# Weight remainders by an accumulating DMA onto a negated rounded copy, and their products last in a tile

## The chip, the cores and the metric

One Trainium2 chip, one of its cores. The time is that of one execution of the whole kernel on the device, in microseconds (us), a median over runs. The engines are called PE (TensorE, the matrix engine, whose weight loads are listed as PEld), DVE (VectorE), ACT (ScalarE), POOL (GpSimd) and SP (SyncE, which issues DMA transfers).

## What is computed

Two layers of a diffusion backbone over 512 latent and 256 context tokens of width 1024. Each layer modulates and normalises its input, projects it once, runs three groups of heads on it (latent attention, neighbourhood attention, a gated DeltaNet that begins with a convolution), projects back, and ends with a gated MLP of hidden width 2816. The last layer keeps only the latent tokens from its mixers on.

```python
h = modulate(rms_norm(x, g_mix[l]), mx[:, 0], mx[:, 1])
mq, mkv, mpe, nq, nk, nv, dn = split_in(h @ w_in[l])
...
x = x + mx[:, 2] * (jnp.concatenate([mla_o, na_o, dn_o], axis=-1) @ w_out[l])
h = modulate(rms_norm(x, g_ffn[l]), mx[:, 3], mx[:, 4])
x = x + mx[:, 5] * swiglu(h, w_gate[l], w_up[l], w_down[l])

def swiglu(h, w_gate, w_up, w_down):
    return (jax.nn.silu(h @ w_gate) * (h @ w_up)) @ w_down
```

Everything is float32.

## The kernel before

PE multiplies in a rounded float32 format (F32R). To keep float32 accuracy each operand is split in two: a rounded copy (hi) and the remainder (lo = value - hi). A product is then three: hi x hi, hi x lo and lo x hi. For weights W and activations X the code calls them wh·xh, wh·xl and wl·xh.

Weights stream through `wtiles` (L202 to L214), one tile of up to 128 x 1024 a call, 208 calls in the program: 48 for the input projection (`w_in`), 4 for the attention's values (`w_nav`), 88 for gate and up (`w_gu`), 48 for the down projection (`w_dn`), 20 for the output projection. A call loads the raw tile (`wr`, two buffers) by a DMA that SP issues, rounds it on ACT into `wh` (L212) and subtracts on POOL into `wl` (L213). `wh` and `wl` have two buffers each; some tiles lie in buffers of their own, `kh` and `kl`. Two tiles of the input projection (`WV`, L48) are subtracted on DVE instead.

`gemm` (L337 to L346) multiplies such a tile: for each set of tokens and each of its (mostly eight) 128-row slices the three products follow one another, wh·xh, wh·xl, wl·xh, all into one accumulator. `proj` (L386) calls it for the input projection's tiles, for one set of tokens at a time. The MLP goes through the hidden width in three parts (`FFN_PARTS`, 8, 7 and 7 blocks of 128). For each block there are a gate and an up tile (accumulators `acc_gu`), then ACT's silu (L1336), DVE's multiplication (L1339), ACT's rounding into `ah` (L1342) and DVE's remainder `al` (L1343). Behind a part's blocks come eight down tiles (`acc_d`), which DVE adds to the residual stream (L1357). In layer 1 a set has 512 tokens, so a gate, up or down tile of 8 slices is 24 matmuls of 128x512.

The DeltaNet's convolution (`conv`) copies an accumulator with borders into `xp` (borders cleared on POOL, L485 to L490), adds four shifted copies on DVE (L497), takes a tanh on ACT (L499) and writes keys, values or queries on DVE (L500, L502, `dn_k` for the keys).

The order on each engine is set by a scheduler with its own simulated times (L1453), not by the order of the code. Each engine then works through its row; an instruction that has to wait holds up all behind it on that engine. A buffer is written again only when its last readers are through.

Of the kernel before, what the change touches and what calls it, by code (L numbers as in the profile page):

```python
# [29 lines left out]
# the last rows of the last down projection: their weights stay for one set of tokens after the other  # L30
# [17 lines left out]
WV = ((6,), (23,))  # L48
# [77 lines left out]
def emit(ctx, tc, a, out, dbg=None):  # L126
# [20 lines left out]
    # the constants: those for the first norm, and the rest, which is loaded behind the first modulation weights  # L147
# [8 lines left out]
    # the first five again for single-pass products, in which they are exact  # L156
# [22 lines left out]
    def preload(after):  # L179
        """the table with both exp and ln, behind the last user of another one"""  # L180
        with tc.issue_after(after.ins):
            S.preload_act_table_set("natural_log_exp_and_others")

    # silu(c), silu(c_ctx), padded to 32 stationary columns
# [3 lines left out]
    # the same as rows  # L188
# [13 lines left out]
    def wtiles(src, n, slot=None, bufs=None, eng=G):  # L202
# [10 lines left out]
        eng.tensor_tensor(out=lo[:, sl], in0=raw[:, sl], in1=hi[:, sl].bitcast(F32), op=ALU.subtract)  # L213
        return hi[:, sl], lo[:, sl]  # L214

    def ada_cols(l, part, j0, nb, bank, sb, slot):
        """nb * 128 modulation rows on the tensor engine: the two conditions stay, the weights stream;
        a quarter of the terms in each column group, summed and turned at the end"""
# [20 lines left out]
    def ada_rows(todo, sb, after):  # L239
        """modulation vectors on the vector engine, one block of 128 rows per step"""  # L240
# [62 lines left out]
    def open_norm(l, side):  # L303
        """the tiles of the input projection's operand, and a set of tokens normed at a time"""
        o = K()
        o.es_h, o.es = ExitStack(), ExitStack()
        hp = pool(o.es_h, f"h{l}", side=side)
        o.hh, o.hl = [[hp.tile([P, T], F32R, name=f"h{x}{k}") for k in range(KD)] for x in "hl"]
        o.sb = pool(o.es, f"sb_n{l}", 2, side=side)
        return o  # L310

    def next_norm(l, xT, bank, side):
        """one set of tokens a step: the norm of the next layer, or the last one"""
# [23 lines left out]
    def gemm(acc, wh, wl, xh, xl, sts, c0=0):  # L337
        """acc[:, st] = W^T x for a [P, nk*128] weight tile over nk activation tiles"""
        nk = len(xh)
        for st in sts:  # L340
            for k in range(nk):
                w = slice(k * P, (k + 1) * P)
                o = acc[:, st.start - c0:st.stop - c0]
                mm(nc, o, wh[:, w], xh[k][:, st], k == 0, False)
                mm(nc, o, wh[:, w], xl[k][:, st], False, False)
                mm(nc, o, wl[:, w], xh[k][:, st], False, k == nk - 1)  # L346

    # ------------------------------------------------------------------ layers
# [10 lines left out]
def layer(tc, nc, a, l, es_x, xT, env, nx):  # L359
# [8 lines left out]
    # the normed input and the residual stream lie on one side, the mixers' data on the other  # L368
# [17 lines left out]
    def proj(t, ctx_too=True, sets=(LAT, CTX)):  # L386
        w, res = early.pop(t, None) or (wtiles(a["w_in"][l, t], 1024, eng=V if t in WV[l] else G), [])
# [20 lines left out]
    else:  # L408
        # the latent tokens of the first projections go ahead of the norm of the context
# [13 lines left out]
    # ------------------------------------------------ input projection  # L423
# [26 lines left out]
    # the latents of the latent attention, split  # L450
# [6 lines left out]
    # bias tables of a pair of heads with the window mask, per kind of query block: [(r c), j, kind, b, kr, c]  # L457
# [49 lines left out]
    # a, b and the rotary key  # L507
# [9 lines left out]
    # ------------------------------------------------ gated DeltaNet: gates and triangular blocks  # L517
# [30 lines left out]
    # cumulative decays  # L548
# [15 lines left out]
    def norms(nm, t_, stat, rk, w_ctx):  # L564
        """sums of squares of q or k per token, and the root's inverse"""
# [34 lines left out]
    # per chunk: Gram matrices and decays; leaves -L packed (forward above the diagonal, backward below)  # L600
    # and the keys decayed to the end of the chunk; the decays wait for the queries where the
    # neighbourhood attention's will be
# [43 lines left out]
    def att_in(x, sb):  # L646
        """the attention matrices of a chunk"""
# [12 lines left out]
    def base_inverse(sb):  # L660
        """(I + L)^-1 of the diagonal 32-blocks, one block per partition: rows of the transposed inverses"""
# [17 lines left out]
    # ------------------------------------------------ the rest of the input projection  # L679
# [14 lines left out]
    # neighbourhood attention: keys, queries (latent ones in blocks of 16 grid columns), values  # L694
# [21 lines left out]
    def do_nav():  # L716
# [13 lines left out]
        # latent values again in blocks of 16 grid columns (r, c): at starts 0, 16, 32, 48 and 8, 24, 40  # L730
# [9 lines left out]
    # the key/value latent is normalised here  # L740
# [15 lines left out]
    # query latent; its row scale is applied to the scores  # L756
    def do_ql():
# [13 lines left out]
        # sml[:, 0:6] = scale * rstd_q per token, sml[:, 6:12] its negative  # L771
# [8 lines left out]
    # 2 silu(z) of the output gate  # L780
# [41 lines left out]
    # ------------------------------------------------ neighbourhood attention, beside the last of the input projection  # L822
# [84 lines left out]
    def inverse(x0, sb, eb):  # L907
        """transposed inverses of two chunks for both directions, joined from 32-blocks: forward and backward
        off-diagonal blocks lie in disjoint places and share the products"""
# [548 lines left out]
```

## Time and profile before

| | us |
|---|---|
| median of 3 runs | 2159.58 |
| lowest and highest | 2149.07, 2163.1 |
| span of the profiled execution | 2157.6 |

| engine | busy us in the profiled execution | share |
|---|---|---|
| PE | 2006.2 | 93% |
| DVE | 1244.7 | 58% |
| POOL | 839.5 | 39% |
| ACT | 708.0 | 33% |

A busy share is an average over stages that have different limits. By the names at work the span divides so (in us from its start): modulation and first norms up to 54; input projection and the DeltaNet's preparation 54 to 378; the rest of the mixers, with the attention heads in 486 to 702; layer 0's MLP 702 to 1242; then layer 1 the same way, 1242 to 1512, 1620 to 1788, 1788 to 2147, and the final norm. A line of the trace gives how long an instruction ran; what stands in square brackets behind it is how long the engine sat idle before, and what released it.

### The profile page before, as it was taken

What the parts mean: (1) busy time and instruction counts of PE and PEld (TensorE: products, weight loads), DVE (VectorE), ACT (ScalarE), POOL (GpSimd) and SP (SyncE); (2) the same over time, 40 slices, a digit from 0 to 9 for tenths busy, and PEclk for the clock granted to TensorE, in tenths of its full rate; (3) what the DMA queues carried; (4) which work ended last, traced back from release to release, by engine and by line L of the source; (5) the groups of instructions that cost most, each with busy time, mean ns of one, the idle gap of its engine ahead of it and who ended that gap; (6) DMA issues with size and microseconds to landing.
All of it is one profiled execution on the core that took longest, in us unless ns stands there. A gap on an engine that the chain in (4) does not pass through costs nothing. (4 is left out here: it accounts for less than half of the span.)

```text
span 2157.6 us, 32133 instructions
## 1 busy us (share of the span) xinstructions
PE 2006.2 (93%) x12770; PEld 1685.9 (78%) x12770; DVE 1244.7 (58%) x2107; ACT 708.0 (33%) x1381; POOL 839.5 (39%) x602
## 2 busy tenths in 40 slices
PE   6899888998999999999999988877999889999998
PEld 4778667887787888888888866766887778888887
DVE  4888963667757457246353368898478753212123
ACT  5433223334534221121122344222434543222233
POOL 3466563103323232322232443856412352444444
PEclk9999998999999999999999999988799999999999
DMA  7424252543312335334432331332523232333332
GB/s 275 81 81 148 72 142 85 156 149 120 103 55 88 108 119 167 97 127 139 125 117 84 128 76 59 124 107 83 132 65 93 72 105 61 98 90 94 100 96 91
DMA packets 119278, 232.57 MB, mean 108 GB/s; under 512 B 30484, under 2 KB 55956, under 8 KB 119000
## 3 DMA queue, kind: packets, MB, share of 16 engines
q1 hardware_dynamic: 119128, 230.51, 35.2%
q8 instruction: 101, 1.65, 0.3%
q14 instruction: 49, 0.40, 0.1%
HBM read 199.46 MB, written 31.01 MB: 107 GB/s over the span
## 5 line engine op out<-in xcount | busy, mean ns | idle before, releaser
L213 POOL TENSOR_TENSOR wl<-wr,wh 128x1024 fp32r<-128x1024 f32 (+2 forms) x188 | 440.6, 2344 | 711.5 <-ACT wh L212 708.5
L212 ACT CAST wh<-wr 128x1024 fp32r<-128x1024 f32 (+2 forms) x190 | 193.5, 1019 | 733.5 <-PE acc_gu L104 285.5
L104 PE MATMUL acc_gu<-fl,wh 128*128 128x512 f32 (+1 forms) x1024 | 360.6, 353 | 5.3 <-DVE fl L301 5.3
L104 PE MATMUL acc_gu<-fh,wh 128*128 128x512 f32 (+1 forms) x1024 | 358.3, 353 | 6.1 <-ACT fh L300 5.3
L104 PE MATMUL acc_gu<-fh,wl 128*128 128x512 f32 (+1 forms) x1024 | 360.1, 352 | 0.0
L104 PE MATMUL acc_in<-hh,wh 128*128 128x512 f32 (+1 forms) x640 | 229.9, 363 | 19.3 <-ACT xp L487 7.7
L104 PE MATMUL acc_in<-hh,wl 128*128 128x512 f32 (+1 forms) x640 | 226.8, 358 | 20.4 <-POOL wl L213 20.4
L104 PE MATMUL acc_in<-hl,wh 128*128 128x512 f32 (+1 forms) x640 | 229.7, 360 | 3.1 <-DVE hl L301 2.0
L1339 DVE TENSOR_TENSOR av<-acc_gu,av 128x768 f32<-128x768 f32 (+1 forms) x44 | 36.3, 825 | 335.8 <-PE acc_gu L104 329.3
L104 PEld LDWEIGHTS acc_gu<-fl,wh 128*128 128x128 f32 x1024 | 193.6, 189 | 34.3 <-DVE fl L301 6.2
L104 PEld LDWEIGHTS acc_gu<-fh,wh 128*128 128x128 f32 x1024 | 192.6, 189 | 35.0 <-ACT fh L300 6.9
L104 PEld LDWEIGHTS acc_gu<-fh,wl 128*128 128x128 f32 x1024 | 193.8, 189 | 27.7
L104 PEld LDWEIGHTS acc_in<-hh,wh 128*128 128x128 f32 x640 | 125.2, 197 | 44.9 <-ACT xp L487 9.4
L104 PE MATMUL acc_d<-al,wh 128*128 128x512 f32 (+1 forms) x444 | 158.0, 356 | 0.0
L104 PE MATMUL acc_d<-ah,wh 128*128 128x512 f32 (+1 forms) x444 | 157.9, 356 | 0.0
L104 PE MATMUL acc_d<-ah,wl 128*128 128x512 f32 (+1 forms) x444 | 156.8, 355 | 0.0
L104 PEld LDWEIGHTS acc_in<-hh,wl 128*128 128x128 f32 x640 | 124.6, 196 | 40.5 <-POOL wl L213 22.5
L250 DVE CUSTOM_DVE_ANT_0 junk<-wada,scb 128x1024 f32<-128x1024 f32 x112 | 145.1, 1295 | 6.9 <-DMA wada<-w_adaT 4.1
L104 PEld LDWEIGHTS acc_in<-hl,wh 128*128 128x128 f32 x640 | 125.8, 197 | 26.4 <-DVE hl L301 4.6
L497 DVE SCALAR_TENSOR_TENSOR cy<-xp,cw,cy 128x770 f32<-128x770 f32 (+1 forms) x96 | 126.0, 1312 | 22.1 <-ACT cy L495 18.4
L1357 DVE SCALAR_TENSOR_TENSOR xT<-acc_d,mod,xT 128x512 f32<-128x512 f32 (+1 forms) x76 | 46.5, 635 | 157.1 <-PE acc_d L104 157.1
L1343 DVE TENSOR_TENSOR al<-av,ah 128x768 fp32r<-128x768 f32 (+1 forms) x44 | 100.5, 2284 | 35.1 <-ACT ah L1342 35.1
(389 smaller groups left out, 4032.2 us busy)
## 6 DMA issues: line engine op xcount, KB each, us to landing
wr<-w_gu SPq DMA_DIRECT2D x88, 512.0 KB, 3.6
wada<-w_adaT SPq DMA_DIRECT2D x56, 512.0 KB, 3.4
wr<-w_in SPq DMA_DIRECT2D x48, 512.0 KB, 3.5
wr<-w_dn SPq DMA_DIRECT2D x32, 448.0 KB, 3.4
wada<-w_ada SPq DMA_DIRECT2D x24, 512.0 KB, 3.4
wada<-w_ada SPq DMA_DIRECT2D x8, 1024.0 KB, 8.7
wr<-w_dn SPq DMA_DIRECT2D x16, 512.0 KB, 3.6
xT<-xT SPq DMA_DIRECT2D x16, 384.0 KB, 5.1
```

Source lines behind the costliest of these rows:

```text
L104: nc.tensor.matmul(out, lhsT, rhs, start=start, stop=stop)
L212: S.copy(out=hi[:, sl], in_=raw[:, sl])
L213: eng.tensor_tensor(out=lo[:, sl], in0=raw[:, sl], in1=hi[:, sl].bitcast(F32), op=ALU.subtract)
L250: V.tensor_tensor_reduce(out=junk, in0=w, in1=scb[:, s], scale=1.0, scalar=0.0, op0=ALU.mult, op1=ALU.add, accum_out=mod[l][:, part, j, s: ...
L497: stt(out=y[:, :wid], in0=xp[:, j:j + wid], scalar=w_(j), in1=y[:, :wid], op0=ALU.mult, op1=ALU.add)
L1339: tt(out=av[:, :nT], in0=accs[1][:, :nT], in1=av[:, :nT], op=ALU.mult)
L1343: after.append(tt(out=l_[:, :nT], in0=av[:, :nT], in1=h_[:, :nT].bitcast(F32), op=ALU.subtract))
L1357: stt(out=xT[:, m, st_], in0=acc, scalar=mod[l][:, 5, m, s:s + 1], in1=xT[:, m, st_], op0=ALU.mult, op1=ALU.add)
```

## The change

`wtiles` rounds on ACT as before. The remainder is then made in two steps: ACT writes the rounded copy's source once more into the `wl` buffer, in the rounded format and times -1, so that it holds -hi; and a DMA that POOL issues reads the weights from memory a second time and adds them to it, which leaves value - hi. `gemm` now takes all products with `wh` of all its sets of tokens first, and those with `wl` behind them. The choice of an engine for the subtraction (`eng`, `WV`) is gone. Comments that the diff also drops are not shown.

```diff
@@ wtiles
-    def wtiles(src, n, slot=None, bufs=None, eng=G):
+    def wtiles(src, n, slot=None, bufs=None):
...
         S.copy(out=hi[:, sl], in_=raw[:, sl])
-        eng.tensor_tensor(out=lo[:, sl], in0=raw[:, sl], in1=hi[:, sl].bitcast(F32), op=ALU.subtract)
+
+        S.activation(out=lo[:, sl], in_=raw[:, sl], func=AF.Copy, scale=-1.0)
+        G.dma_start(out=lo[:, sl], in_=src, accum_op=ALU.add)
         return hi[:, sl], lo[:, sl]
@@ gemm
         nk = len(xh)
-        for st in sts:
+        W = [slice(k * P, (k + 1) * P) for k in range(nk)]
+        os_ = [(acc[:, st.start - c0:st.stop - c0], st) for st in sts]
+        for o, st in os_:
             for k in range(nk):
-                w = slice(k * P, (k + 1) * P)
-                o = acc[:, st.start - c0:st.stop - c0]
-                mm(nc, o, wh[:, w], xh[k][:, st], k == 0, False)
-                mm(nc, o, wh[:, w], xl[k][:, st], False, False)
-                mm(nc, o, wl[:, w], xh[k][:, st], False, k == nk - 1)
+                mm(nc, o, wh[:, W[k]], xh[k][:, st], k == 0, False)
+                mm(nc, o, wh[:, W[k]], xl[k][:, st], False, False)
+        for o, st in os_:
+            for k in range(nk):
+                mm(nc, o, wl[:, W[k]], xh[k][:, st], False, k == nk - 1)
@@ proj
-        w, res = early.pop(t, None) or (wtiles(a["w_in"][l, t], 1024, eng=V if t in WV[l] else G), [])
+        w, res = early.pop(t, None) or (wtiles(a["w_in"][l, t], 1024), [])
```

What the scheduler makes of it shows in the rows of the engines. On PE, in layer 1's MLP, before: `acc_gu` is an accumulator, `fh` and `fl` are the slices of the normed activations, and the number behind a name is that of the tile. The end of one gate/up tile and the start of the next:

```order
L104 MATMUL acc_gu_17850<-fl7_16168,wh_17845 128x512
L104 MATMUL acc_gu_17850<-fh7_16160,wl_17846 128x512
L104 MATMUL acc_gu_17881<-fh0_16153,wh_17876 128x512 [waits DVE_49,Activation_49]
L104 MATMUL acc_gu_17881<-fl0_16161,wh_17876 128x512
L104 MATMUL acc_gu_17881<-fh0_16153,wl_17877 128x512 [waits Pool_49]
L104 MATMUL acc_gu_17881<-fh1_16154,wh_17876 128x512
```

The same engine and place now:

```order
L103 MATMUL acc_gu_18108<-fh7_16300,wh_18102 128x512
L103 MATMUL acc_gu_18108<-fl7_16308,wh_18102 128x512
L103 MATMUL acc_gu_18037<-fh0_16293,wl_18032 128x512 [waits DMASW2_49]
L103 MATMUL acc_gu_18037<-fh1_16294,wl_18032 128x512
L103 MATMUL acc_gu_18037<-fh2_16295,wl_18032 128x512
...
L103 MATMUL acc_gu_18037<-fh7_16300,wl_18032 128x512
L103 MATMUL acc_gu_18140<-fh0_16293,wh_18134 128x512 [waits DVE_49,Activation_49]
```

A tile's eight `wl` products (18037) now stand behind the sixteen `wh` products of the tile after it (18108), and wait for a DMA instead of POOL. In layer 0's MLP they stand behind the `wh` products of their own tile.

On ACT, in the same stage, before (`av` is the silu of a gate tile, `ah` the rounding of its product with the up tile):

```order
L212 CAST wh_17876<-wr_17875 128x1024 [waits DMAHW6_49,PE_49,Pool_49]
L212 CAST wh_17914<-wr_17913 128x1024 [waits DMAHW7_49,PE_49,Pool_49]
L1336 ACTIVATE av_17906<-acc_gu_17850 128x512 [waits PE_49]
L212 CAST wh_17945<-wr_17944 128x1024 [waits DMAHW0_49,PE_49,Pool_49]
L1342 CAST ah_17909<-av_17906 128x512 [waits DVE_49]
```

And now:

```order
L211 CAST wh_18134<-wr_18133 128x1024 [waits DMAHW0_49,Activation_49]
L1340 ACTIVATE av_18094<-acc_gu_18037 128x512 [waits PE_49]
L213 ACTIVATE wl_18103<-wr_18101 128x1024 [waits DMASW2_49]
L211 CAST wh_18173<-wr_18172 128x1024 [waits DMAHW1_49,Activation_49]
L213 ACTIVATE wl_18135<-wr_18133 128x1024 [waits DMASW3_49,PE_49]
L1346 CAST ah_18097<-av_18094 128x512 [waits DVE_49]
```

A negated copy (L213) stands behind each rounding, and waits until PE is through with the tile that had the buffer before. The silu of a gate tile stands ahead of one of them.

On POOL, in layer 0's input projection, before (`gul` belongs to the DeltaNet's gates, `xp` is the convolution's input):

```order
L627 TENSOR_TENSOR gul_992<-cst2_61,g_l_960 128x512
L485 MEMSET xp_813 128x2 [waits DVE_49,Activation_49,Pool_49]
L486 MEMSET xp_813 128x2
L490 MEMSET xp_813 128x2
L213 TENSOR_TENSOR wl_1011<-wr_1009,wh_1010 128x1024 [waits DMAHW0_49,PE_49,Activation_49]
L485 MEMSET xp_885 128x2 [waits DVE_49,Activation_49,Pool_49]
```

And now:

```order
L631 TENSOR_TENSOR gul_997<-cst2_61,g_l_965 128x512
L489 MEMSET xp_817 128x2 [waits DVE_49,Activation_49,Pool_49]
L490 MEMSET xp_817 128x2
L494 MEMSET xp_817 128x2
L214 DMA wl_1016<-w_in 128x1024 [waits DMASW3_49,Activation_49]
L489 MEMSET xp_890 128x2 [waits DVE_49,Activation_49,Pool_49]
```

The issue of the accumulating DMA has the place that the subtraction had.

## Rows read from the trace of the kernel before

**Rows 1.** The page's head and its first section: busy time by engine.

```profile
span 2157.6 us, 32133 instructions
PE 2006.2 (93%) x12770; PEld 1685.9 (78%) x12770; DVE 1244.7 (58%) x2107; ACT 708.0 (33%) x1381; POOL 839.5 (39%) x602
```

**Rows 2.** Windows by stage: start:end, length, busy time (instructions) per engine, granted clock, DMA.

```profile
core 0: us, PE busy (x) PEld busy (x) DVE busy (x) ACT busy (x) POOL busy (x), PEclk, DMA share, GB/s
54.00:378.00 324.00, 286.41 (x1793) 241.79 (x1792) 243.00 (x344) 103.39 (x180) 172.95 (x149) 0.93 0.36 102
486.00:702.00 216.00, 196.03 (x1256) 161.04 (x1254) 149.99 (x312) 98.72 (x251) 69.36 (x55) 0.94 0.28 91
702.00:1242.00 540.00, 540.00 (x3122) 472.55 (x3121) 254.05 (x342) 117.57 (x136) 163.04 (x73) 1.00 0.39 121
1242.00:1512.00 270.00, 224.91 (x1161) 181.54 (x1160) 216.62 (x300) 90.55 (x153) 156.29 (x136) 0.92 0.31 90
1620.00:1788.00 168.00, 149.47 (x1020) 125.77 (x1020) 117.89 (x240) 79.65 (x211) 58.83 (x53) 0.96 0.28 85
1788.00:2147.00 359.00, 359.00 (x1672) 298.79 (x1671) 96.97 (x95) 106.23 (x149) 155.00 (x72) 1.00 0.30 90
```

**Rows 3.** Waits of PE: who waited for whom, us in total, times, longest.

```profile
PE acc_in L104 <- POOL wl L213: 20.4, 5, 9.0
```

**Rows 4.** The page's costliest groups: the subtraction; count | busy, mean ns | idle before, releaser.

```profile
L213 POOL TENSOR_TENSOR wl<-wr,wh 128x1024 fp32r<-128x1024 f32 (+2 forms) x188 | 440.6, 2344 | 711.5 <-ACT wh L212 708.5
```

**Rows 5.** Windows by stage of line 213 alone, the subtraction: DVE, then POOL.

```profile
54.00:378.00 324.00, 1.22 (x1) 57.45 (x23) 0.93 0.36 102
486.00:702.00 216.00, 0.00 (x0) 30.55 (x14) 0.94 0.28 91
1242.00:1512.00 270.00, 0.00 (x0) 53.25 (x22) 0.92 0.31 90
1620.00:1788.00 168.00, 0.00 (x0) 26.01 (x12) 0.96 0.28 85
1788.00:2147.00 359.00, 0.00 (x0) 148.76 (x64) 1.00 0.30 90
```

**Rows 6.** Timeline of DVE, 82 to 110 us: start, duration, instruction, idle before.

```profile
81.42 0.69 DVE L500 SCALAR_TENSOR_TENSOR dn_k<-th,cy 128x512 f32<-128x512 f32 x1 [1.89 <-ACT th L499]
...
90.49 2.37 DVE L500 SCALAR_TENSOR_TENSOR dn_k<-th,cy 128x512 f32<-128x512 f32 x1 [0.92 <-ACT th L499]
...
98.28 0.69 DVE L500 SCALAR_TENSOR_TENSOR dn_k<-th,cy 128x512 f32<-128x512 f32 x1 [0.91 <-ACT th L499]
```

**Rows 7.** Timeline of POOL in the same stretch.

```profile
89.91 2.40 POOL L213 TENSOR_TENSOR wl<-wr,wh 128x1024 fp32r<-128x1024 f32 x1
```

**Rows 8.** Timeline of POOL in layer 1's MLP, two tiles.

```profile
1843.85 2.39 POOL L213 TENSOR_TENSOR wl<-wr,wh 128x1024 fp32r<-128x1024 f32 x1 [3.06 <-ACT wh L212]
1849.29 2.39 POOL L213 TENSOR_TENSOR wl<-wr,wh 128x1024 fp32r<-128x1024 f32 x1 [3.05 <-ACT wh L212]
```

**Rows 9.** Timeline of ACT in the same stretch.

```profile
1842.72 1.05 ACT L212 CAST wh<-wr 128x1024 fp32r<-128x1024 f32 x1 [3.84 <-PE acc_gu L104]
1843.68 0.59 ACT L1336 ACTIVATE av<-acc_gu 128x512 f32<-128x512 f32 x1
```

**Rows 10.** Timeline of DVE in the same stretch.

```profile
1848.42 0.69 DVE L1339 TENSOR_TENSOR av<-acc_gu,av 128x512 f32<-128x512 f32 x1 [7.07 <-PE acc_gu L104]
1849.80 2.44 DVE L1343 TENSOR_TENSOR al<-av,ah 128x512 fp32r<-128x512 f32 x1 [0.69 <-ACT ah L1342]
```

**Rows 11.** DMA issues of the page: count, KB each, median us from issue to landing.

```profile
wr<-w_gu SPq DMA_DIRECT2D x88, 512.0 KB, 3.6
```

**Rows 12.** Line 213 by form: durations in ns (least/median/most), first and last start.

```profile
L213 DVE TENSOR_TENSOR wl<-wr,wh x2: 1220/1222/1225, 66.6 to 1518.5; 128x1024 fp32r<-128x1024 f32 x2
```

**Rows 13.** Chain that ended last, in order of time: a stretch of gate/up matmuls, start, length.

```profile
1914.87 76.18 PE acc_gu L104 x336
```

More of the change, by code (lines that the diff above doesn't have):

```diff
@@ L47 @@
 INV = ((3, 4), (5, 2))
-WV = ((6,), (23,))
 MR = 2
```

## The prediction, made before the changed kernel ran

> **What bounds the kernel now.** I read the busy shares first [rows 1]: PE is at work 93% of 2157.6 us, so about 151 us are left in which another engine can matter. Next the same by stage [rows 2]. In the two gated-MLP stages (702 to 1242 and 1788 to 2147) PE is busy all the time; the reader is to see that nothing can be gained there, only lost. In the two stages of the input projection and the DeltaNet preparation (54 to 378 and 1242 to 1512) PE is idle for 37.6 and 45.1 us, and the engine busy most beside it is DVE, 243.0 of 324 and 216.6 of 270 us (0.75 and 0.80). The two attention stages leave 20.0 and 18.5 us of PE idle with DVE at 0.69 and 0.70. Last the waits of PE [rows 3]: 20.4 us for the subtracted remainder, in five waits, the largest single entry.
>
> The subtraction itself is cheap to look at: 188 of them, 2.34 us each, with POOL idle 711.5 us ahead of them, nearly all of it for ScalarE's rounding [rows 4]. POOL as an engine is no bound. What the subtraction does to others is seen where DVE meets it [rows 6, 7]: the same DVE instruction (128x512 into `dn_k`) takes 0.69 us at 81.42 and at 98.28, but 2.37 us at 90.49, and in between POOL subtracts from 89.91 to 92.31. DVE was held up by 1.68 us and went on when POOL was done.
>
> **What the change removes.** Per tile one POOL subtraction. In the two DVE-heavy stages there are 23 + 22 = 45 of them [rows 5]. A DVE instruction that comes at a random moment of a 2.4 us subtraction is held up by half of it, 1.2 us, and DVE has work at hand for about 0.78 of the time, so one subtraction costs DVE 1.2 x 0.78 = 0.94 us, and 45 cost 42 us. Bounds: nothing (DVE catches up while it would wait anyway), and 45 x 1.68 = 76 us, which is about all that PE idles there. I take two thirds of 42, 28 us, since DVE sets the pace in most of these stages but not at their beginnings. In the attention stages 14 + 12 = 26 subtractions cost DVE 26 x 1.2 x 0.69 = 21.5 us; there the softmax chain goes round several engines, and I take one third, 7 us. In the MLP stages DVE is slack and its relief is worth nothing.
>
> **What it adds on ScalarE.** One more pass per tile, as long as the rounding, 1.05 us [rows 9]: 208 x 1.05 = 218 us on an engine that is busy 708 of 2157.6 us [rows 1]. Between the units of the MLP it is hidden by idle time: three ScalarE instructions there leave 3.8 us of every 5.44 free. In the DVE-heavy stages it stands ahead of the `tanh` for which DVE waits 0.9 us at a time [rows 6]: 45 x half of 1.05 x ScalarE's share 0.33 x the same two thirds comes to 5 us.
>
> **What it adds on the DMA.** Each tile is now read a second time, by a DMA that POOL issues and that adds into the negated copy. No row of before shows such a DMA. Its duration D, from issue to landing, is bounded by rows: below by the plain load of 512 KB, 3.6 us [rows 11]; above by three of these one after the other (read the source, read the destination, write), 10.8 us. I take 3.6, plus the same bytes moved once more for the destination, plus the same again because the next raw load runs beside it. One load fills all the engines for 0.30 x 5.44 = 1.6 us (share of the last MLP stage [rows 2], one tile in 5.44 us [rows 8]), so D = 3.6 + 1.6 + 1.6 = 6.8 us, nearer to the lower bound.
>
> **What it moves.** The wl products stand after all wh products of their tile, and in layer 1's MLP after those of the next tile too, so D has room. A matmul takes 76.18 / 336 = 0.2267 us [rows 13]. There are two wl buffers: from the end of one tile's wl products to the start of those that use the same buffer again, PE goes through wh of a tile (16), wl of another (8), wh of the next (16), 40 x 0.2267 = 9.07 us. The negated copy takes 1.05 of them, and before it the silu of a gate tile 0.59 [rows 9]. So D may be 8.0 us, or 7.4 behind a silu, and 6.8 fits: cost 0. Without that cover the price is steep: a buffer's round is copy 1.05, D, and its own wl products 8 x 0.2267 = 1.81, for two tiles. Past D = 8.0 each us more costs half a us for each of 64 tiles [rows 5], 32 us. Layer 0's MLP has 768 tokens per tile and so half as much room again.
>
> Two places get less cover. At the change from gate/up to down in the second and third part of layer 1, only two matmuls stand between the last gate/up product and the first that needs `al`; DVE's multiply and its remainder are 0.69 and up to 2.44 us [rows 10], so about 2 us each, 4 us in all, up to 9. And the 20.4 us of waits for wl [rows 3]: the DMA is later than POOL was (6.8 against 2.4), but wl is needed 16 matmuls, 3.6 us, later. I leave them as they are.
>
> POOL's issues: behind them stand the clearing of `xp`'s borders and the small products of the gates, which waited for ScalarE behind the subtraction already. POOL's own 440 us go away; what writing a DMA's description costs it no row shows, and I bound it by 0 and the 2.34 us that it replaces, off the path in either case. SP issues what it did.
>
> **A rule that speaks against it.** DVE's and POOL's mutual hold-up [rows 6, 7] is the row. The Trainium skill, "SBUF — State Buffer", section "SBUF: two separate sides", says that a DMA issued from the GpSimd queue has its descriptors written by GpSimd, which cannot write them while VectorE runs an operation in a two-port mode, so that the transfer seems blocked by that operation; no DMA in this trace comes from that queue, so no run here shows it yet.
>
> **The sum.** 28 + 7 gained, 5 and 4 lost: 26 us. The profiled execution's span is 2157.6, about 2 us under the median of 2159.6: 2157.6 - 26 + 2 = 2133.6 us.
>
> **The rivals.** *B, the accumulating DMA paces layer 1's MLP.* If adding costs three passes, D is 10.8: the round is 1.05 + 10.8 + 1.81 = 13.66 for two tiles, 6.83 each against 5.44, 64 x 1.39 = 89 us lost there: 2133.6 + 89 = 2223. It eats the whole gain of 26 from D = 8.8 on. For it: the transfer is the one thing not seen, and PE has no slack there. Against it: the engines are only 0.30 busy [rows 2], and all moved bytes doubled or tripled still fit. Chance 0.26. *C, DVE's hold-up is not on the path.* The stages idle for chains (conv, norm, gates), and DVE makes up for it; then only the 7 us, less 9 of costs: 2162. For it: of PE's waits only some name DVE, and the longest names POOL, whose replacement is longer. Chance 0.17. *D, DVE holds up POOL's DMAs.* The DMA that falls on the `al` remainder, one in two gate/up tiles, comes up to 2.44 us late [rows 10]: D = 9.2, the round 12.1 for two tiles against 10.88, 1.2 us for each of about 20 pairs, 24 us: 2133.6 + 24 = 2158. Against it: 2.44 us is itself a remainder that met a subtraction (POOL from 1849.29, DVE from 1849.80 [rows 8, 10]); DVE takes 1.22 us for twice the width [rows 12], so it would shrink to about 0.6. Chance 0.09. [...]
>
> **How the numbers follow.** My forecast has 0.48, with its own range 2095 (all of the 42 + 21.5 comes back) to 2150. A measurement here tells about 1% from no change: 2138 and 2181. Faster: the forecast's part below 2138, 0.42. Same: its rest 0.06, most of C and half of D, and a mild B, 0.30. Slower: the rest of B, C and D, 0.28. The range goes from 2095 to B's 2225.
>
> **What would show it.** Right: in the stages 54 to 378 and 1242 to 1512 DVE's conv instructions at their short durations, both stages shorter by some 14 us each, `al` near 0.6 us, the last MLP stage still 359 us with PE full, and the DMA landing within 8.0 us. Wrong: PE waiting for the DMA into wl in the last MLP stage, landings above 8.0 us there, or the two DVE-heavy stages as long as before with DVE now idle.

## The result, and the profile after

The changed kernel takes 2235.1 us (median of 4 runs, 2225.59 to 2238.8) against 2160.7 for the kernel before on the same chip: 1.036 times as long, 95% interval 1.0329 to 1.0382. The forecast was 2133.6 us in a range of 2095 to 2225. It was wrong in sign, and the time lies above the range. (The 2160.7 is a median of 4 runs, the three shown ahead of the prediction and one more.) One execution, 2207.9 us of e10 below, ran in a slower state of the chip at a granted clock of 0.944 and is left out.

The head of the page after, its first section, the queue of POOL's DMAs and the issues of the gate/up weights:

```profile
span 2230.7 us, 32485 instructions
PE 2044.9 (92%) x12770; PEld 1697.6 (76%) x12770; DVE 1112.8 (50%) x2105; ACT 902.8 (40%) x1589; POOL 530.3 (24%) x604
q0 software_dynamic: 29952, 104.87, 26.9%
wr<-w_gu SPq DMA_DIRECT2D x88, 512.0 KB, 3.9
wl<-w_gu POOLq DMA_DIRECT2D x84, 512.0 KB, 7.8
```

Beside [rows 1], DVE has lost 132 us of busy time, POOL 309, and ACT has gained 195, all as meant; yet the span is 73 us longer. The accumulating DMA takes 7.8 us from issue to landing where 6.8 was forecast. PE has the same 12770 products as before and is busy 39 us longer with them.

Where the time went is read from windows cut at the first gate/up product and the last down product of each layer. Of the kernel before, then of the changed one (columns as in [rows 2]):

```profile
0.00:682.00 682.00, 605.86 (x4575) 501.19 (x4576) 470.21 (x914) 260.94 (x600) 270.82 (x242) 0.95 0.38 118
682.00:1239.00 557.00, 555.45 (x3178) 484.19 (x3178) 271.84 (x368) 123.03 (x149) 164.74 (x74) 0.99 0.39 123
1239.00:1772.00 533.00, 474.66 (x3295) 392.18 (x3293) 388.94 (x708) 208.51 (x466) 238.78 (x207) 0.93 0.32 91
1772.00:2147.00 375.00, 368.80 (x1723) 307.75 (x1722) 109.50 (x113) 113.58 (x165) 161.78 (x76) 0.99 0.30 89
```

```profile
0.00:692.00 692.00, 609.89 (x4574) 501.72 (x4574) 439.25 (x913) 296.34 (x640) 212.19 (x244) 0.95 0.54 145
692.00:1249.00 557.00, 555.39 (x3177) 484.44 (x3178) 230.01 (x367) 190.47 (x214) 64.15 (x73) 1.00 0.73 184
1249.00:1794.00 545.00, 488.77 (x3295) 401.17 (x3293) 370.92 (x708) 242.44 (x507) 186.11 (x211) 0.90 0.50 123
1794.00:2220.00 426.00, 389.44 (x1724) 309.68 (x1724) 68.49 (x113) 171.85 (x226) 64.86 (x76) 0.97 0.71 157
```

Layer 0's MLP is as long as before. Layer 1's MLP is 50 us longer, and the two stretches ahead of the MLPs, where 35 us were to be gained, are 10 and 12 us longer, although DVE has 49 us less to do in them.

PE loses this time in two ways, by standing idle and by working more slowly. In layer 1's MLP it idles 30 us more than before (length less busy time) and is busy 21 us more. In the stretch ahead of that MLP it idles 56 us, before 58; its 3295 products take 14 us longer, at a mean granted clock of 0.90 against 0.93. How the two ways hang together is seen at one place (timeline of PE in the changed kernel, first part of layer 1's MLP): PE idles 4.0 us for an accumulating DMA, and the eight products behind it, at 1878.52, take 3.79 us where eight such take 2.0 to 2.1. The granted clock from 1878.5 to 1884 is 0.50, the lower (1.2 GHz) of its two levels. There the wait cost more than its own length. How much of the 39 us comes about in this way was not followed.

What paces the second and third part of layer 1's MLP stands on the chain of work that ended last (start, length, what):

```profile
1963.24 1.06 ACT wl L213
1964.30 0.02 issue
1964.32 5.07 DMA wr<-w_gu
...
1969.49 1.04 ACT wh L211
1970.53 0.50 ACT av L1340
1971.03 0.96 ACT wl L213
...
1972.00 3.92 DMA wr<-w_gu
...
1976.95 1.06 ACT wl L213
...
1978.03 3.72 DMA wr<-w_gu
```

Neither PE nor the accumulating DMA is in it. The negated copy of one tile ends, 20 ns later a raw load starts, the rounding follows the landing, the next negated copy follows the rounding, and the next load follows that. In the chain of before this stretch was matmuls alone [rows 13]. The rows on ACT, printed with the change, say why. The copies of `wr_18101` and `wr_18133` are of neighbouring tiles, and between them stands the rounding of `wr_18172`, the tile after both. That tile has to be loaded into the buffer that the first copy sets free, and the second copy can't overtake the rounding that waits for this load. So the two raw buffers never load at the same time; they work as one. Copies start at 1963.24, 1970.93 and 1976.95, 6.9 us apart on average and 6.3 over the whole second part (1944.3 to 2025.9, 13 tiles), where PE's products of a tile take 5.44.

In the first part of the same MLP it is the accumulating DMA that the chain goes through:

```profile
1855.37 7.92 DMA wl<-w_gu
...
1863.34 2.12 PE acc_gu L103 x8
...
1865.49 3.59 issue
...
1869.09 9.38 DMA wl<-w_gu
...
1878.52 3.79 PE acc_gu L103 x8
...
1884.28 8.11 DMA wl<-w_gu
```

That is the prediction's round of a wl buffer (DMA, its eight products, silu and copy), here 13.7 and 15.2 us for two tiles against 10.88. The 3.59 us that the chain calls issue hold more than silu and copy: a rounding stands ahead of them on ACT, and it had waited until 1866.20 for its raw load.

### The profile page after: what moved, and what is told of

It is laid out like the page before. It is cut to its first block, busy times and chain, and to the rows that moved or that the text cites. A ratio compares the mean times of both kernels' runs of the same rounds, so it can differ in the third digit from the quotient of the medians.

```text
span 2230.7 us, 32485 instructions
## 1 busy us (share of the span) xinstructions
PE 2044.9 (92%) x12770; PEld 1697.6 (76%) x12770; DVE 1112.8 (50%) x2105; ACT 902.8 (40%) x1589; POOL 530.3 (24%) x604
## 3 DMA queue, kind: packets, MB, share of 16 engines
q0 software_dynamic: 29952, 104.87, 26.9%
## 4 chain that ended last, share of the span: by engine, by line
PE 57%; DMA 16%; DVE 12%; issue 6%; ACT 6%; POOL 1%; SPq 1%; DVEq 0%; ACTq 0%; POOLq 0%
PE acc_gu L103 18%; PE acc_d L103 10%; PE acc_in L103 7%; PE acc_o L103 5%; DMA wr<-w_gu 4%; DVE cy L501 2%; DMA wl<-w_gu 2%; DMA wl<-w_dn 2%; ACT wl L213 2%; DVE tmp L677 2%; PE pp L103 1%; PE s_mla L103 1%; PE o_mla L103 1%; PE s_na L103 1%; DMA wl<-w_in 1%
## 5 line engine op out<-in xcount | busy, mean ns | idle before, releaser
L103 PE MATMUL acc_gu<-fh,wh 128*128 128x512 f32 (+1 forms) x1024 | 348.1, 357 | 23.2 <-ACT wh L211 12.6
L103 PE MATMUL acc_gu<-fl,wh 128*128 128x512 f32 (+1 forms) x1024 | 344.7, 355 | 0.0
L103 PEld LDWEIGHTS acc_gu<-fh,wh 128*128 128x128 f32 x1024 | 194.1, 190 | 61.7 <-ACT wh L211 23.2
L213 ACT ACTIVATE wl<-wr 128x1024 fp32r<-128x1024 f32 (+2 forms) x190 | 194.9, 1026 | 93.9 <-PE acc_gu L103 51.1
L103 PE MATMUL acc_in<-hh,wh 128*128 128x512 f32 (+1 forms) x640 | 219.8, 363 | 14.1 <-ACT wh L211 5.4
L103 PE MATMUL acc_in<-hl,wh 128*128 128x512 f32 (+1 forms) x640 | 218.8, 360 | 3.8 <-POOL hl L299 2.4
L103 PE MATMUL acc_gu<-fh,wl 128*128 128x512 f32 (+1 forms) x1024 | 210.0, 354 | 8.3 <-DMA wl<-w_gu 8.2
L214 POOL DMA_DIRECT2D wl<-w_gu x84 | 73.1, 870 | 573.7 <-ACT wl L213 525.6
L103 PEld LDWEIGHTS acc_gu<-fh,wl 128*128 128x128 f32 x1024 | 169.1, 189 | 39.4 <-DMA wl<-w_gu 11.8
L103 PE MATMUL acc_in<-hh,wl 128*128 128x512 f32 (+1 forms) x640 | 143.4, 365 | 15.1 <-DMA wl<-w_in 15.1
L103 PEld LDWEIGHTS acc_in<-hh,wl 128*128 128x128 f32 x640 | 110.0, 202 | 36.3 <-DMA wl<-w_in 17.7
L677 POOL TENSOR_TENSOR tmp<-R,Bk 96x1 f32<-96x1 f32 (+30 forms) x62 | 84.9, 1369 | 82.0 <-DVE R L678 71.5
```

Of the source, the lines that this page charges most:

```text
L103: nc.tensor.matmul(out, lhsT, rhs, start=start, stop=stop)
L213: S.activation(out=lo[:, sl], in_=raw[:, sl], func=AF.Copy, scale=-1.0)
L214: G.dma_start(out=lo[:, sl], in_=src, accum_op=ALU.add)
L677: (V if d == 0 else G).tensor_tensor(out=t_, in0=R[:, d, js, js], in1=bc1(Bk[:, js, i], s), op=ALU.mult)
```

## The experiments

Each ran beside the kernel before on the same chip, where that took 2156.6 to 2157.2 us (2160.7 beside the changed kernel); the ratio is to that. Changing the source also lets the scheduler order the rows anew, so only e6, whose rows stayed in the same order, differs from its parent in one thing alone. Lengths of the four stretches (start to layer 0's MLP, that MLP, from there to layer 1's MLP, that MLP), in us, by the first gate/up and last down products of one profiled execution each:

| kernel | to MLP 0 | MLP 0 | to MLP 1 | MLP 1 | time, median | ratio to before (95%) |
|---|---|---|---|---|---|---|
| before | 681.8 | 557.0 | 532.8 | 375.5 | 2160.7 | |
| changed | 692.0 | 557.1 | 544.8 | 425.9 | 2235.1 | 1.0329 to 1.0382 |
| e1_from_hi | 696.7 | 557.0 | 527.6 | 377.5 | 2165.1 | 1.0019 to 1.0053 |
| e5_no_dma | 661.3 | 555.3 | 498.0 | 369.1 | 2097.6 | 0.9722 to 0.9751 |
| e3_order_only | 675.2 | 559.0 | 542.7 | 375.6 | 2166.5 | 1.0039 to 1.0069 |
| e4_dma_only | 715.6 | 621.6 | 565.9 | 561.6 | 2475.8 | 1.1461 to 1.1559 |
| e6_plain_dma | 676.7 | 555.1 | 532.9 | 390.8 | 2168.4 | 1.0039 to 1.0080 |
| e9_mlp_only | 678.4 | 557.8 | 543.8 | 376.3 | 2168.5 | 1.0042 to 1.0072 |
| e10_both_sets | 687.5 | 554.7 | 538.1 | 375.4 | 2181.8 | 1.0064 to 1.0148 |
| e11_proj_only | 694.9 | 557.7 | 506.3 | 374.5 | 2147.8 | 0.9947 to 0.9996 |
| e12_layer1_proj | 673.8 | 557.6 | 522.2 | 374.9 | 2138.7 | 0.9847 to 0.9924 |
| e14_rest_old | 680.1 | 556.9 | 515.5 | 375.7 | 2144.4 | 0.9914 to 0.9962 |
| e13_unread_sub | 682.6 | 558.5 | 542.5 | 373.3 | 2168.4 | 1.0032 to 1.0062 |
| e15_no_sub | 661.3 | 558.4 | 505.6 | 372.7 | 2111.6 | 0.9756 to 0.9800 |

**e1, the raw buffer freed by the rounding.**

```diff
-        S.activation(out=lo[:, sl], in_=raw[:, sl], func=AF.Copy, scale=-1.0)
+        S.activation(out=lo[:, sl], in_=hi[:, sl].bitcast(F32), func=AF.Copy, scale=-1.0)
```

> The changed kernel, but the negated copy is made from the rounded tile wh, not from the raw tile, so that the rounding alone releases the raw buffer. Theory R (the raw buffers pace parts 2 and 3 of layer 1's MLP: the negated copy holds the raw tile until PE is through with the wl products two tiles back, and the next rounding stands between the two copies on ACT, so a load of 3.8 us, a rounding and a copy follow one another for each tile, over 6 us against 5.44): a gate/up tile there goes back to about 5.44 us, 33 us less or some 40 with the down tiles: about 2195 us; the waits of the rounding for the raw load in that stage fall from 123 us to under 40. Theory D (the accumulating DMA's 7.8 us pace it): no change, 2235 us, the same 6.4 us per tile.

2165.1 us, 70 us less than the changed kernel and 30 less than R named. The edit is one operand, but the scheduler also ordered ACT anew: in the second and third part of MLP 1 two negated copies now follow one another without a rounding between them (timeline of ACT in e1):

```profile
1952.45 1.05 ACT L213 ACTIVATE wl<-wh 128x1024 fp32r<-128x1024 f32 x1
1955.18 1.06 ACT L213 ACTIVATE wl<-wh 128x1024 fp32r<-128x1024 f32 x1 [1.68 <-issue]
```

So this run does not part the operand from the order that came with it. MLP 1 is back at 377.5. The waits of ACT in that stage (who for whom, us, times, longest), first of the changed kernel, then of e1:

```profile
ACT wh L211 <- DMA wr<-w_gu: 123.2, 31, 6.8
ACT wh L211 <- DMA wr<-w_dn: 46.7, 13, 4.8
```

```profile
ACT wh L211 <- PE acc_gu L103: 37.4, 18, 4.8
ACT wl L213 <- PE acc_gu L103: 28.8, 13, 3.3
```

The rounding no longer waits for a load at the top of the list, but for PE: there is slack again. Its waits for gate/up loads fall from 123.2 to 3.7 us, where R said under 40, and the chain of that MLP has no such load in it. That is what theory R said of the second and third part. The accumulating DMA became shorter too (median of all 5.8 us, before 7.7, from the last lines below), so this run alone can't part R from D; e6 is made for that.

```profile
DMA to landing us min/median/max: 5.1/7.7/12.3
```

```profile
DMA to landing us min/median/max: 4.4/5.8/11.5
```

**e6, the same rows on every engine, but a plain DMA.**

```diff
-        G.dma_start(out=lo[:, sl], in_=src, accum_op=ALU.add)
+        G.dma_start(out=lo[:, sl], in_=src)
```

> The changed kernel with a plain DMA from POOL in place of the accumulating one, so that wl holds the raw weights and the result is not the reference's. It prices the adding: if reading the destination back costs, the landing falls from 7.7 us to 5 or less; if the software queue and the raw load beside it are what takes the time, it stays above 7. Theory R (raw load, rounding and copy in one line, because the next rounding stands between two copies on ACT): parts 2 and 3 of layer 1's MLP keep over 5.9 us per gate/up tile however short the landing is, and the time stays above 2200 us. Theory D: with a landing under 6 us that MLP returns to 377 us, as in the run with the copy from wh, and the time to about 2165 us.

All engines have the rows of the changed kernel in the same order here, so only the DMA differs. Its landing and its queue:

```profile
DMA to landing us min/median/max: 3.5/4.5/8.8
q0 software_dynamic: 29952, 104.87, 14.1%
```

The adding costs 3.2 us of landing (medians of all 208 transfers, 384 to 512 KB; for the 512 KB of `wl<-w_gu` it is 7.8 against 4.4), and nearly doubles the DMA engines' time for the same bytes (26.9% of 2230.7 us against 14.1% of 2166.4, 1.96 times). In time it costs 64 us between the two profiled executions: 15, 2, 12 and 35 us in the four stretches. That is most of what the changed kernel lost against the kernel before.

MLP 1 falls to 390.8 us, no further, though this DMA lands 4.5 us after its issue. By the three parts of that MLP (from the first gate/up product of one to that of the next), e6 is 10.1 us shorter than the kernel before in the first and 10.6 and 14.8 longer in the second and third; the changed kernel is 1.9, 18.7 and 29.8 longer. So in the last two parts 25 of the 48.5 us are lost without any adding. The timeline of ACT shows the same sequence:

```profile
1930.44 1.04 ACT L211 CAST wh<-wr 128x1024 fp32r<-128x1024 f32 x1 [3.67 <-DMA wr<-w_gu]
1936.26 1.05 ACT L211 CAST wh<-wr 128x1024 fp32r<-128x1024 f32 x1 [3.31 <-DMA wr<-w_gu]
1942.51 1.05 ACT L211 CAST wh<-wr 128x1024 fp32r<-128x1024 f32 x1 [3.61 <-DMA wr<-w_gu]
```

6.0 us per tile, where R said over 5.9. At this pace the silu of a gate tile, which stands ahead of every second copy and waits for PE's products, is in the line too: the chain of the third part goes copy, load, rounding, 24 products, silu, copy, with loads at 2042.42, 2054.65 and 2066.50, 12 us for two tiles. The other 35 us of MLP 1 come with the adding: 12 in the first part, whose chain goes through the accumulating DMA, and 23 in the others, where the raw loads of gate/up tiles land later (median of all 88 in the kernel 3.9 us, up to 5.1 in the chain above, against 3.5 in e6). So neither theory holds alone: the raw buffers make the line, the accumulating DMA lengthens what stands in it. The time, 2168.4, is below the 2200 us that R named and near the 2165 of D, but not for D's reason: MLP 1 stays 15 us long, and the stretches ahead of the MLPs gained 15 and 12 us.

**e5, no DMA at all.**

```diff
-        G.dma_start(out=lo[:, sl], in_=src, accum_op=ALU.add)
```

> The changed kernel without the accumulating DMA: wl is left as the negated rounded copy, so the remainder is missing from the result. Theory R: parts 2 and 3 of layer 1's MLP stay above 5.9 us per gate/up tile, since copy, load and rounding are all still there (a little faster, as the loads run alone at 3.6 us); only the first part and the waits of PE for wl improve: about 2205 us. Theory D: all of layer 1's MLP goes back to 375 us: 2185 us or less.

2097.6 us, faster than the kernel before by 2.6%, and every stretch is shorter. So the relief that was the point of the prediction is there when nothing is added, and no cost of the second pass on ACT is seen beside it (the run does not price the pass by itself). The rows are in another order than the changed kernel's, so the 137 us between the two are not all the DMA's own. R's statement on the MLP failed, for a reason that its own mechanism gives: without the DMA the scheduler orders ACT otherwise. A negated copy is followed by the rounding of the very next tile, not of the one after, and both raw buffers load in turn (tiles counted along ACT's row in the trace; copies at 1900.97 and 1905.97; the part's 336 gate/up products take 76.18 us in its chain, as before). The copy still reads the raw tile here. So that operand alone does not make the line; it takes the rounding that stands between two copies.

**e13 and e15, what the subtraction costs.** For the input projection's tiles (`w_in`, `w_nav`), in the new order with POOL's subtraction:

```diff
-        return hi[:, sl], lo[:, sl]
+        return hi[:, sl], (lo if late else hi)[:, sl]     # late is False for w_in and w_nav
...
+        if late:                                          # e15 only
             eng.tensor_tensor(out=lo[:, sl], in0=raw[:, sl], in1=hi[:, sl].bitcast(F32), op=ALU.subtract)
```

> New order, subtraction on POOL, but PE multiplies by wh a second time where the input projection's tiles would use wl: the subtraction runs and nobody reads it, so the remainder's products are wrong there. It tells what the subtraction costs: theory H (DVE held up by POOL): the cost stays, 2150 to 2166 us; theory L (PE is served late by POOL): it goes, 2100 to 2115 us.

> As the one before without the subtraction of the input projection's tiles. Theory H and L: 2095 to 2115 us, the bound of what taking the subtraction away can bring; the difference to the run with the unread subtraction is DVE's hold-up alone, 35 us by the prediction's reckoning for these tiles (28 of the two preparation stages and some of the 7), under 10 by theory L.

With a subtraction that nobody reads the time is that of the order alone, 2168.4; without it 2111.6. These 52 subtractions (50 on POOL, two on DVE) cost 57 us merely by running. Theory L (PE served late) is out. DVE's busy time shows the hold-up; the two stretches ahead of the MLPs of e13, then of e15:

```profile
0.00:683.00 683.00, 602.21 (x4575) 501.04 (x4576) 464.82 (x913) 258.96 (x599) 267.42 (x242) 0.95 0.37 118
1241.00:1784.00 543.00, 474.92 (x3295) 393.85 (x3293) 386.81 (x708) 208.80 (x470) 243.66 (x209) 0.92 0.30 90
```

```profile
0.00:661.00 661.00, 594.75 (x4574) 494.83 (x4574) 433.16 (x912) 258.86 (x599) 214.87 (x217) 0.96 0.39 122
1220.00:1725.00 505.00, 461.24 (x3291) 382.02 (x3289) 367.85 (x707) 208.18 (x470) 184.77 (x185) 0.95 0.32 96
```

The same 1621 DVE instructions (within two) take 464.8 + 386.8 = 851.6 us beside the subtractions and 801.0 without them, 50.6 us less, of which 2.4 are DVE's own two subtractions. The convolution's sums into `cy` give 22.0 of it and DVE's steps of the DeltaNet's inverse 14.4. By the same rows PE's idle time falls by 39 us and its busy time by 21, at granted clocks of 0.96 and 0.95 against 0.95 and 0.92: so not even all of DVE's 50 us came back as PE's idle time, and a third of the gain is products that ran faster. Nor need the rest be DVE alone: the subtractions also stand between POOL's own steps of the DeltaNet's inverse, as in this timeline of POOL in e13 (L676 is the inverse's product):

```profile
300.92 2.44 POOL L676 TENSOR_TENSOR tmp<-R,Bk 96x841 f32<-96x841 f32 x1 [1.08 <-DVE R L677]
303.31 2.40 POOL L213 TENSOR_TENSOR wl<-wr,wh 128x1024 fp32r<-128x1024 f32 x1
305.67 2.62 POOL L676 TENSOR_TENSOR tmp<-R,Bk 96x900 f32<-96x900 f32 x1
308.25 2.40 POOL L213 TENSOR_TENSOR wl<-wr,wh 128x1024 fp32r<-128x1024 f32 x1
```

DVE's waits for these steps of POOL's, ahead of its own reduction, are 22.9 us in e13 and 10.4 in e15.

**e3 and e4, the two halves of the change.** e3 is the kernel before with the changed `gemm`; e4 is the changed kernel with the `gemm` of before.

> The kernel before with the new order of products alone (all wh products first), the remainder still subtracted on POOL. If PE's waits for the subtraction (20.4 us) were worth their length and are covered by the 16 products ahead: about 2142 us. If they only move elsewhere, because DVE and the chains set these stages: 2155 to 2162 us. In either case layer 1's MLP keeps its 375 us.

> The changed kernel with the old order of products (wh, wh, wl for each slice): the accumulating DMA without its cover. A wl buffer's round is then copy 1.05, DMA 7.8 and a whole tile of 24 products, 5.44, for two tiles: 7.1 us per tile in layer 1's MLP against 5.44, 64 tiles, +109 us, and about +20 in layer 0's MLP: 2290 us, if the DMA's duration matters at all (theory D, and R with it). If the products' order hides nothing: 2235 us.

The order alone costs 0.5%. PE's waits for POOL fall from 20.4 to 11.2 us, as they should, but PE then waits for other things (20.7 us for the copies into `xp`), and the stretch to MLP 1 is 10 us longer; which reordering does that was not followed. The accumulating DMA without its cover costs 15%, and more than reckoned (2290 us); why it is more was not followed. MLP 1 goes to 561.6 us, and PE's waits name the DMA (waits of PE in e4):

```profile
PE acc_gu L103 <- DMA wl<-w_gu: 99.0, 48, 5.5
PE acc_d L103 <- DMA wl<-w_dn: 51.0, 19, 4.5
PE acc_in L103 <- DMA wl<-w_in: 43.4, 16, 8.5
```

So the DMA needs the order, and the order gains nothing by itself.

**e9, e11, e10, where it helps.** In e1's form, `acc=True` (copy and accumulating DMA) for some tiles and POOL's subtraction for the rest: e9 all but `w_in` and `w_nav`, e11 those two alone. e10 is e1 with the `wh` products of both sets of tokens ahead of all `wl` products in `proj`:

```diff
+        if acc:
             S.activation(out=lo[:, sl], in_=hi[:, sl].bitcast(F32), func=AF.Copy, scale=-1.0)
             G.dma_start(out=lo[:, sl], in_=src, accum_op=ALU.add)
+        else:
+            G.tensor_tensor(out=lo[:, sl], in0=raw[:, sl], in1=hi[:, sl].bitcast(F32), op=ALU.subtract)
```

```diff
-                gemm(res[-1][1], *w, hh, hl, (cols,), cols.start)
+                new.append(res[-1])
+        for cols, acc in new:      # wh x hh, wh x hl of both sets
...
+        for cols, acc in new:      # then wl x hh of both sets
```

> The copy from wh and the accumulating DMA for the output projection and the MLP; the input projection's tiles (w_in, w_nav) are subtracted on POOL as before. The MLP gained and lost nothing with the copy from wh (377.5 against 375.5 us), so if the loss of that kernel (8 us) and its gain both lie in the input projection: 2160 us, as with the new order alone (2166) or up to 6 us less.

> The opposite split: copy from wh and accumulating DMA for the input projection's tiles alone, subtraction on POOL for the output projection and the MLP. If the two parts do not interact, this and the opposite split together differ from the new order alone (2166) by as much as the kernel with both (2165) does: about 2165 us here. If the accumulating DMAs of the input projection are late because the DMA engines or POOL's row are busy, it shows here too: PE's waits for wl<-w_in stay at 25 us.

> The kernel with the copy from wh, and in the input projection the wh products of both sets of tokens (16 of 128x512 and 16 of 128x256) ahead of both sets' wl products, 5.4 us of cover for a tile's own DMA in place of 3.6 us. If PE's waits for wl<-w_in (25.3 us) are what eats the relief of DVE: they halve and the time falls to 2140 to 2150 us. If the waits come from copies and DMAs that start late, by the order on ACT and POOL: within 6 us of 2165.

e9 takes as long as the order alone, so in the MLP the new way is neutral once the raw buffer is free. e11 is 17 us below the 2165 expected, so the halves do not simply add up; PE's waits for `wl<-w_in` stay near the 25 us named (23.2). It gains in layer 1 (506.3 us to its MLP against 532.8) and loses in layer 0 (694.9 against 681.8). e10 met neither expectation: its runs lie between 2168 and 2187 us, 0.6 to 1.5% above the kernel before, and PE's waits for `wl<-w_in` did not halve but grew from 25.3 to 30.7 us. More products ahead of the `wl` products did not shorten the waits in this order of rows; the run does not say what would.

**e12 and e14, put together.** e12 is e11 with `acc=l == 1`, so that layer 0 keeps POOL's subtraction; e14 also gives everything but layer 1's input projection the old order of products back.

> New order everywhere; copy from wh and accumulating DMA for layer 1's input projection alone (24 + 2 tiles), subtraction on POOL elsewhere. Stages by the runs so far: up to the MLP of layer 0 675 us (new order alone), layer 0's MLP 557, layer 1 up to its MLP 506 (the run with the input projection's tiles alone), its MLP 376, and 10 at the end: 2124 us, faster than both kernels, if stages add up. If a schedule of one layer carries over into the other, or 506 was luck of that schedule: 2145 to 2165.

> As the one before, but everything other than layer 1's input projection in the old order of products. Layer 0 up to the MLP as before (682 us): 2130 us if stages add up, 2145 to 2165 if not.

e12 takes 2138.7 us, 1.1% less than the kernel before (0.8 to 1.5%), and beats both kernels; e14, 2144.4, 0.6% less. The stages add up only in part: e12 missed the 2124 us, as layer 1 took 522 us to its MLP, not e11's 506, and e14 missed its 2130. In e12 the DMA is still what PE waits for longest (waits of PE):

```profile
PE acc_in L103 <- DMA wl<-w_in: 20.2, 4, 11.0
```

Two direct tests of the raw buffers' line were not run: a third raw buffer in the changed kernel, and the changed kernel with ACT's order of e5.

## Why the prediction was wrong, point by point

**The relief of DVE and POOL** was right in kind and too small. 35 us were taken; e13 and e15 give 57 for the input projection's tiles alone. The hold-up per tile was well judged: 42 + 21.5 us of DVE time forecast for 71 tiles, 0.89 each; 48.2 measured for the 50 on POOL, 0.96 each. Too small were the factors for the path (two thirds, one third): PE's idle time alone fell by 39 us, about four fifths of DVE's. Two things were not in the sum at all: that PE's products ran faster when it idled less (21 us), and POOL's steps of the inverse, for which DVE waits, under "no bound".

**The pass on ACT**, 5 us, does not show as busy time that costs (e5); its place in ACT's row and the tile that it reads do, below. The rows read for it hold two ACT instructions per tile of 5.44 us, not three, so the pass leaves 2.8 us free there, not 3.8. `al` fell as forecast: its mean goes from 2284 to 826 ns over 44 instructions, and 0.69 us for 128x512.

**The duration of the DMA**, 6.8 us, was 7.8: the term for the destination was taken as 1.6 us and measured 3.2 for the adding (e6 against the changed kernel). The other two terms, a plain load with another beside it, were taken as 5.2 and measured 4.5.

Of the 101 us between forecast and measurement, 46 lie in layer 1's MLP (50 us longer, where 4 were forecast) and 52 in the two stretches ahead of the MLPs (22 us longer, where 30 less were forecast). A step of the prediction failed for each.

**"So D may be 8.0 us, or 7.4 behind a silu, and 6.8 fits: cost 0"** is the step that failed in layer 1's MLP. The reckoning followed the wl buffers and stopped there. It missed that the negated copy also reads the raw tile. Before, the raw tile was free when POOL had subtracted; now it is free only after the copy. And ACT's row puts a rounding between two copies: it waits for a load into the buffer that the first copy frees, and the copy that would free the other buffer stands behind it. In the second and third part a copy behind gate/up products waited for PE only twice (6.1 us), but the roundings of gate/up tiles waited for their loads 27 times (105.4 us): it is the order on ACT that holds the raw tile, not the wl buffer. Both facts, what the copy reads and where it stands, were in the rows of ACT in the section on the change. Cost: 50 us in MLP 1, by its parts 1.9, 18.7 and 29.8 us. The bound of 8.0 us for D was too loose besides: with D at 7.8 the adding alone cost 35 us there (e6), where by the step it should have cost nothing. e1 takes nearly all of the 50 back.

**Rival B**, the accumulating DMA as the pace of layer 1's MLP, named the place and nearly the time (2223). But by its condition, D above 8.8 us, it would not have happened: D was 7.8 in the median. Only the chain of the first part of that MLP went its way. That the time came near 2223 is luck: other losses added up to it.

**"I leave them as they are"**, of the waits for wl, is the step that failed ahead of the MLPs. From e15, which has neither subtraction nor DMA for these tiles, to the changed kernel the two stretches grow by 31 and 39 us. With a plain DMA (e6) they are already 15 and 27 us longer than in e15, and the adding, with the same rows, brings another 15 and 12. The chain of the changed kernel goes through the DMA in places, such as:

```profile
86.78 7.61 DMA wl<-w_in
231.40 6.01 DMA wl<-w_in
288.03 5.57 DMA wl<-w_in
1308.32 7.10 DMA wl<-w_in
```

These four are 26 us. The second starts when POOL is through with a step of the inverse (229.59, 1.81 us in the chain): the issue had to wait there behind POOL's arithmetic. Beside the adding other transfers land later too: the raw loads of the input projection after 5.0 us in the median, against 3.5 in the kernel before and in e6. PE's direct waits for `wl<-w_in` are only 15.1 us, and of the 71 us by which the windows of e15 and of the changed kernel differ only 28 are PE's idle time. The other 43 are the same products running longer, 15 us in the first stretch and 28 in the second, at granted clocks of 0.95 and 0.90 against 0.96 and 0.95. How the part that a plain DMA already costs comes about stays open: e15 and e6 differ in the order of their rows as well.

**Rival C**, DVE's hold-up off the path, does not stand: leaving out the subtractions gave 57 us (e13, e15), though not through DVE alone. **Rival D**, DVE holding up the DMAs, finds no support: the `al` remainder shrank to 0.69 us, and the DMA's shortening from 7.7 to 4.5 us came from leaving out the adding, with DVE's row unchanged. The Trainium skill, "SBUF — State Buffer", section "SBUF: two separate sides", speaks of such a hold-up by VectorE operations in a two-port mode. No run here shows one, and none was made for it alone.

**The transitions**, 4 us: PE waited 3.1 us in two waits for `ah` in MLP 1. Not reckoned were its waits for the down tiles' own DMAs, 4.9 us and, for the kept tiles at the end, 4.5.

## What to carry to other kernels

When a step is taken over by another instruction, follow every buffer that the new instruction reads as well as the one it writes, and look at what stands between it and its twin on its engine's row: here taking an operand from the rounded tile instead of the raw one, with the order of rows that came of it, was worth 70 us. An engine with a low busy share can still cost through those it holds up, so the price of such work is best taken by running it unread and then leaving it out. A transfer that replaces arithmetic should be checked for cover at every place where the chain is short, not only in the steady state. And when a stretch grows, compare PE's busy time as well as its idle time: the same products can simply run longer.

## What the runs showed of the hardware

An accumulating DMA took 3.2 us longer to land than a plain one with the same rows around it (medians of 208 transfers, 7.7 against 4.5), and 1.96 times the DMA engines' time. The Trainium skill, "Collectives: The Full Stack", section "The bandwidth ceiling: the fold count and why AG ≠ RS ≠ AR", says of a collective's reduce step that it is slow not because the add costs cycles but because the add reads two sources, and gives a measured ratio of 1.93 to a step that only copies. The 1.96 here is near that; what the transfer read no run here shows. A subtraction of 2.40 us on POOL stretched a DVE instruction from 0.69 to 2.37 us [rows 6, 7], and 52 subtractions cost 57 us of the whole time (e13, e15). In the changed kernel PE idled 4.0 us up to 1878.5 and then had a granted clock of 0.50 for 5.5 us. POOL is busy 0.87 us for each issue (73.1 us for 84 of them), a third of the subtraction it replaced:

```profile
L214 POOL DMA_DIRECT2D wl<-w_gu x84 | 73.1, 870 | 573.7 <-ACT wl L213 525.6
```
